# Decoder step on one Trainium2 core: squares folded to one tile, output tiles rescaled on VectorE, normalised tiles made in portions

## The chip, the core and the metric

The kernel runs on one core of a Trainium2 chip. Five engines work side by side, each with its own queue: TensorE (PE; its weight loads are listed apart as PEld) multiplies matrices into PSUM, VectorE (DVE), ScalarE (ACT) and GpSimd (POOL) do elementwise work, and SyncE (SP) issues the DMAs. An engine works off its queue in order and waits at an instruction until its inputs are there and its output buffer is free. The metric is the device time of one execution in microseconds (us); the profile shows one execution.

## The reference

One step of a decoder layer for 256 prompt tokens and 8 x 4 sample tokens, 288 tokens in all, with 2048 features. What matters here is the first half:

```python
mod = (silu(c) @ w_ada + b_ada)            # per request: sh_m, sc_m, gt_m, sh_f, sc_f, gt_f
h = rms(x, g_mix) * (1 + sc_m) + sh_m      # rms: x * rsqrt(mean(x*x) + EPS) * gain
proj = h @ w_in                            # 2048 -> 9216 columns (72 tiles of 128)
b_gate, c_gate, hc, u, v, ga, gb = split(proj)
...
```

Behind that come a short convolution, a spatial gate, a merge through three more weight matrices, a second rms and a SwiGLU of width 5632. Everything is float32.

## The kernel before, in words

Activations lie with features on the 128 partitions and the 288 tokens along the free axis: 16 tiles of x, one for each 128 features. For precision each operand is split into a high part (`hi`, a cast on ScalarE) and a low part (`lo`, a subtraction on VectorE), and each product is made of three matmuls (`triple`, L217 to L219). Weight blocks come by DMA into seven buffers `raw`, and `Blk.split` (L390 to L406) makes hi and lo of four 128x128 tiles at a time into four buffers each.

The product with w_in is done in passes over parts of the 16 contraction tiles. Blocks `wA` (nine, each eight output tiles) take tiles 0 and 1 for all 72 outputs; `wB` tiles 2 to 4 and `wX` tiles 5 to 7 for outputs 48 to 71; `wC` (24 blocks, two outputs each, six contraction tiles) tiles 2 to 7 for outputs 0 to 47; `wD` the last eight tiles. The partial sums are kept in SBUF and added to by the sinks (`sinkA` to `sinkD`), which also free the PSUM buffer of the output tile; there are four such buffers.

The root of the mean square isn't known when the first pass starts. So the first ROOTLESS = 32 outputs are made from x times (1 + sc_m) x gain, without the root (`mk_xe`, `xe`), with ten more columns: the shift and scale vectors `mod` as nine columns and one of padding, 298 in all (`TU`). Once the root is known (`S["rb1"]`, the root spread over the partitions), these 32 tiles are multiplied by it and get the shift of their sample requests (`rescale`, on POOL); the shift of the prompt is added in `sinkC`. Outputs from 32 on use `h1`, which contains the root.

The modulation `mod` comes from `Ada` blocks (aA: contraction over w_ada, four blocks of 1 MB; aC, aD, aE in between the others later). Ahead of them and between them stand idle matmuls (`warm`) on a constant tile.

`squares1` squares x in five pieces on ScalarE and adds them on VectorE down to six tiles of 288 tokens. `sums1` sums each over the partitions by matmuls with a column of ones (L514), three for each tile, and `roots` makes the root. `norm1` spreads it (L206, L527) and makes h1[0] and h1[1] at once (`mk_h1(0, 2)`). The squares' instructions are hung up in a table of slots (i, j), "after output tile j of block wA[i]", which `paced` works off, with the splits of the next weights in its even slots. `later(f, gap)` puts work behind a number of `triple`s.

The order on TensorE is the program's throughout. On ScalarE, VectorE and SyncE it is the program's until `head.close()` at wA[3]; behind that a planner sets the order of all engines but TensorE. SyncE issues loads in order, seven blocks ahead. Each load waits there until its buffer is free.

Of the kernel before, what the change touches and what calls it, by code (L numbers as in the profile page):

```python
# [1 line left out]

# [1 line left out]

# [16 lines left out]
NC = 9  # L21
# [22 lines left out]


TB = (0, 128, 160)
ROOTLESS = 32
LATER = 48
XCUT = (0, 2, 6, 10, 14, 16)

# [35 lines left out]
def _body(tc, nc, d, pc, pw, pslot, ptmp, pps):  # L86
# [289 lines left out]
    class Blk(Step):  # L376
# [10 lines left out]

        cut, width, outer, pace = None, T, False, None

        def split(self, most=99):  # L390
            n = self.nk * self.nm
            nseg = -(-n // SEG)
            per = -(-n // nseg)
            self.parts = self.parts or []
            for s in range(len(self.parts), n, per):
                if most == 0:
                    return
                most -= 1
                e = min(n, s + per)
                w = (e - s) * 128  # L400
                hi = pw.tile([P, w], F32R, tag="hi", name=nm("hi"), bufs=SPB, padded_shape=[P, SEG * 128])
                A.copy(hi, self.raw[:, s * 128 : e * 128])  # L402
                lo = pw.tile([P, w], F32R, tag="lo", name=nm("lo"), bufs=SPB, padded_shape=[P, SEG * 128])
                V.tensor_tensor(lo, self.raw[:, s * 128 : e * 128], hi.bitcast(F32), ALU.subtract)  # L404
# [73 lines left out]
    def warm(n):  # L478
        for _ in range(n):
            PE.matmul(idle[:, :T], wb[:, :P], wb, start=True, stop=True)  # L480

    def squares1():
        qa, qb = (pw.tile([P, 2048], F32, tag="raw", name=nm("q"), bufs=RAW) for _ in range(2))
        for q in (qa, qb):
            G.memset(q[:, 7 * T : 7 * T + 1], 0.0)

        def part_of(q, o, n):
            return q[:, o * T : (o + n) * T].rearrange("p (k t) -> p k t", t=T)

        q1, q0, q2, q4 = part_of(qa, 0, 4), part_of(qa, 4, 2), part_of(qb, 0, 4), part_of(qb, 4, 2)  # L490

        def square(q, i):
            return lambda: A.activation(q, x[:, XCUT[i] : XCUT[i + 1], :], AF.Square)

        def add(o, q):
            return lambda: V.tensor_tensor(o, o, q, ALU.add)
# [12 lines left out]
    def sums1():  # L509
        got = S["r1"] = {"ps": psmisc()}  # L510
        qs = S.pop("sq")
        for i, q in enumerate(qs):
            for tb, o in enumerate(TB):
                PE.matmul(  # L514
                    got["ps"][:, tb : tb + 1],
                    q[:, o : o + 128],
                    ones[:, 0:1],
                    start=i + tb == 0,
                    stop=False,
                    skip_group_check=True,  # L520
                )
        roots(got, D, False, False)

    def norm1():
        ps = rstd_bcast(S["r1"])
        S["rb1"] = ptmp.tile([P, T], F32, tag="rb", name=nm("rb"), bufs=1)
        A.copy(S["rb1"], ps)  # L527
        mk_h1(0, 2, False).run()

    h1, xe = {}, {}  # L530

    def mk_xe():
        end = tmp(2 * (TU - TP)).rearrange("p (k t) -> p k t", k=2)
        V.memset(end[:, :, T + NC - TP :], 0.0)

        def scaled(k):
            hi = slot(F32R, (P, TU))
            A.activation(hi[:, :TP], x[:, k, :TP], AF.Copy, scale=gm1[:, k, 0:1])
            lo = slot(F32R, (P, TU))
            xe[k] = (hi, lo)  # L540

        def ends(k):
            V.tensor_tensor(sam(end[:, k, : T - TP]), sam(x[:, k, TP:]), bc4(gm1[:, k, 1:]), ALU.mult)
            V.tensor_copy(end[:, k, T - TP : T - TP + NC], mod[:, k, :])
            V.tensor_copy(xe[k][0][:, TP:], end[:, k, :])
# [8 lines left out]
        def weights(n):  # L554
            wA[0].split(n)
# [30 lines left out]
    def sinkA(m, ps):  # L586
        t = slot(shape=(P, TU) if m < ROOTLESS else (P, T))
        part[m] = t[:, :T]
        w = T
        if m < ROOTLESS:  # L590
            raws[m], w = t, TU
        if m % 2:
            A.copy(t[:, :w], ps[:, :w])  # L593
        else:
            V.tensor_copy(t[:, :w], ps[:, :w])  # L595

    def rescale(m0, m1):
        def f():
            for m in range(m0, m1):
                t = raws[m]  # L600
                G.tensor_tensor(t[:, :T], t[:, :T], S["rb1"], ALU.mult)  # L601
                G.tensor_tensor(sam(t[:, TP:T]), sam(t[:, TP:T]), bc4(t[:, T + 1 : T + NC]), ALU.add)

        return Do(f, None)

    def sinkC(m, ps):
        if m not in raws:
            return sinkB(m, ps)
        t = raws.pop(m)
        V.scalar_tensor_tensor(t[:, :TP], ps[:, :TP], t[:, T : T + 1], t[:, :TP], ALU.add, ALU.add)  # L610
        V.tensor_tensor(t[:, TP:T], ps[:, TP:T], t[:, TP:T], ALU.add)

    def sinkB(m, ps):
        V.tensor_tensor(part[m], ps[:, :T], part[m], ALU.add)  # L614


    ya, yb, u2 = {}, {}, {}
# [18 lines left out]
    def mix_conv(j):  # L636
        b, c, hc = part.pop(j), part.pop(8 + j), part.pop(16 + j)
        z = tmp()
        V.tensor_tensor(z, c, hc, ALU.mult)
# [3 lines left out]
        V.tensor_copy(zs[:, :, 0:2], state[:, j])  # L643
# [203 lines left out]
    wX = [Blk("wX", i, rh1, lambda m, ps: sinkB(LATER + m, ps)) for i in range((72 - LATER) // 4)]  # L847
# [23 lines left out]
    plan = {2: [Do(root, None)], 6: aC[:4], 8: aC[4:] + [mk_h1(2, 5)]}  # L871
    for i in range(4):
# [52 lines left out]
    load_x(0)  # L925
    stream[4].load(512)
    S["paced"] = squares1()
    stream[5].load()
    load_x(1)
    load_x(2)  # L930
    stream[6].load()
    load_x(3)
    load_x(4)
    SY.dma_start(cp, d["cpack2"])
    blks = [s for s in stream if isinstance(s, Blk)]
    nxt, cur = 0, 0
    for s in steps:
        if s is wA[3]:
            head.close()
        if isinstance(s, Do):  # L940
            if pending and s.gap is not None:
# [130 lines left out]
```

## Time and profile before

| what | us |
|---|---|
| median of three runs | 1662.79 (1661.29 to 1664.73) |
| the profiled execution, as timed | 1665.84 |
| its span, first to last instruction | 1664.0 |
| TensorE busy | 1643.4 |
| VectorE busy | 998.5 |
| ScalarE busy | 740.1 |
| POOL busy | 59.5 |

The span is what the profile divides into shares; the timed figure of the same execution holds 1.84 us more around it. A busy TensorE need not be one at full rate, since matmuls overlap and its clock can be granted at half; the views by stretches therefore give the granted clock with each stretch. In the rows of a timeline the first two numbers are start and duration in us; what stands in brackets is the idle time ahead and what ended it. In a line's own view the three numbers are least, median and most ns of one instruction.

### The profile page before, as it was taken

How to read it: one execution, taken by the hardware profiler on the slowest of the kernel's cores; microseconds unless marked ns; L12 is line 12 of the kernel's file. 1: busy time of each engine (PE TensorE's matmuls, PEld its weight loads, DVE VectorE, ACT ScalarE, POOL GpSimd, SP SyncE). 2: the span in 40 equal slices, each digit the busy share in tenths (PEclk: the TensorE clock that was granted, in tenths of full speed). 3: DMA queues.
4: the chain of work that ended last, by engine and by line, in shares of the span. 5: the costliest groups of instructions: out<-in, count | busy, mean ns of one | idle time of the engine just before them, and what ended most of it. 6: DMA issues, size and time to landing. Idle time of an engine off the chain costs nothing.

```text
span 1664.0 us, 31217 instructions
## 1 busy us (share of the span) xinstructions
PE 1643.4 (99%) x12466; PEld 1568.3 (94%) x12466; DVE 998.5 (60%) x2087; ACT 740.1 (44%) x1355; POOL 59.5 (4%) x128
## 2 busy tenths in 40 slices
PE   9999999999999999999999999999999999999997
PEld 7888989999989998999989999999999999999997
DVE  4567656877755566567844455555555555555565
ACT  4344334653434434446734444444444444344453
POOL 0720000000000000002000000000000000000000
PEclk9899999999999999999999999999999999999998
DMA  9478776766688656764477546453464534644341
GB/s 349 143 302 322 299 294 208 266 250 253 255 306 317 242 215 253 283 223 162 146 299 304 207 157 220 155 175 120 157 221 163 174 117 156 217 173 164 115 154 57
DMA packets 59281, 357.59 MB, mean 215 GB/s; under 512 B 6624, under 2 KB 9600, under 8 KB 28288
## 3 DMA queue, kind: packets, MB, share of 16 engines
q1 hardware_dynamic: 58848, 355.38, 58.7%
q8 instruction: 97, 1.59, 0.4%
q14 instruction: 48, 0.39, 0.1%
q10 hardware_dynamic: 288, 0.22, 0.1%
HBM read 352.49 MB, written 3.09 MB: 214 GB/s over the span
## 4 chain that ended last, share of the span: by engine, by line
issue 51%; PE 46%; DVE 2%; ACT 0%; POOL 0%; POOLq 0%; DVEq 0%; ACTq 0%
PE pm L217 13%; PE pm L218 13%; PE pm L219 13%; PE ada L333 4%; PE pm L480 1%; DVE lo L404 1%; PE px L514 0%; DVE x L828 0%; PE px L358 0%; ACT hi L402 0%; DVE s L269 0%; DVE s L250 0%; PE px L715 0%; PE px L717 0%; PE px L675 0%
## 5 line engine op out<-in xcount | busy, mean ns | idle before, releaser
L217 PE MATMUL pm<-s,hi 128*128 128x288 f32 (+1 forms) x3760 | 1113.6, 296 | 6.0 <-ACT s L593 4.4
L218 PE MATMUL pm<-s,hi 128*128 128x288 f32 (+1 forms) x3760 | 1110.2, 295 | 0.5 <-DVE s L269 0.3
L219 PE MATMUL pm<-s,lo 128*128 128x288 f32 (+1 forms) x3760 | 1110.4, 295 | 0.0
L404 DVE TENSOR_TENSOR lo<-raw,hi 128x512 fp32r<-128x512 f32 (+1 forms) x960 | 658.8, 687 | 504.3 <-ACT hi L402 489.9
L402 ACT CAST hi<-raw 128x512 fp32r<-128x512 f32 (+1 forms) x960 | 587.8, 613 | 816.4 <-PE pm L218 793.6
L217 PEld LDWEIGHTS pm<-s,hi 128*128 128x128 f32 x3760 | 708.5, 188 | 25.8 <-issue 16.1
L218 PEld LDWEIGHTS pm<-s,hi 128*128 128x128 f32 x3760 | 707.7, 188 | 1.4 <-DVE s L552 0.7
L219 PEld LDWEIGHTS pm<-s,lo 128*128 128x128 f32 x3760 | 708.0, 188 | 0.0
L333 PE MATMUL ada<-raw,cs 128*32 128x512 f32 (+2 forms) x832 | 88.2, 563 | 0.0
L333 PEld LDWEIGHTS ada<-raw,cs 128*32 128x32 f32 x832 | 24.2, 109 | 46.1 <-issue 44.5
L197 POOL TENSOR_TENSOR r<-e,mhalf 128x3 f32<-128x3 f32 x4 | 3.4, 855 | 1149.5 <-DVE e L196 1102.5
L622 DVE TENSOR_TENSOR s<-pm,s 128x288 f32<-128x288 f32 x72 | 32.9, 457 | 15.7 <-PE pm L219 15.6
L614 DVE TENSOR_TENSOR s<-pm,s 128x288 f32<-128x288 f32 x64 | 29.1, 455 | 19.2 <-PE pm L219 17.9
L245 DVE TENSOR_TENSOR s<-t,s 128x288 fp32r<-128x288 f32 (+1 forms) x76 | 34.6, 459 | 6.9 <-ACT s L243 6.9
L243 ACT CAST s<-t 128x288 fp32r<-128x288 f32 (+1 forms) x76 | 32.6, 433 | 13.6 <-DVE t L654 6.4
L285 DVE SCALAR_TENSOR_TENSOR x<-pm,mod,x 128x256 f32<-128x256 f32 x80 | 38.0, 475 | 0.0
L601 POOL TENSOR_TENSOR s<-s,rb 128x288 f32<-128x288 f32 x32 | 29.3, 916 | 4.2 <-ACT rb L527 4.2
L800 DVE SCALAR_TENSOR_TENSOR t<-t,pm 128x288 f32<-128x288 f32 x42 | 19.1, 454 | 16.7 <-PE pm L219 16.7
L284 DVE TENSOR_TENSOR t<-pm,mod 128x32 f32<-128x32 f32 x80 | 15.3, 192 | 21.2 <-PE pm L219 21.2
L595 DVE COPY s<-pm 128x288 f32<-128x288 f32 (+1 forms) x36 | 16.2, 456 | 12.1 <-PE pm L219 12.1
L156 ACT ACTIVATE t<-x 128x288 f32<-128x288 f32 x30 | 13.3, 445 | 20.8 <-DVE x L286 20.8
L593 ACT COPY s<-pm 128x288 f32<-128x288 f32 (+1 forms) x36 | 14.2, 399 | 16.8 <-PE pm L219 16.8
(119 smaller groups left out, 495.7 us busy)
## 6 DMA issues: line engine op xcount, KB each, us to landing
raw<-in_fi SPq DMA_DIRECT2D x84, 1024.0 KB, 4.8
raw<-in_a SPq DMA_DIRECT2D x64, 1024.0 KB, 9.7
raw<-in_f SPq DMA_DIRECT2D x64, 704.0 KB, 4.1
raw<-in_wD SPq DMA_DIRECT2D x36, 1024.0 KB, 4.9
raw<-in_wC SPq DMA_DIRECT2D x24, 768.0 KB, 5.1
raw<-in_aE SPq DMA_DIRECT2D x16, 1024.0 KB, 9.7
raw<-in_wo SPq DMA_DIRECT2D x16, 1024.0 KB, 4.9
raw<-in_pa SPq DMA_DIRECT2D x8, 1024.0 KB, 4.9
```

What stands on the lines that cost most here:

```text
L217: PE.matmul(out, wh, ah, start=first, stop=False)
L218: PE.matmul(out, wh, al, start=False, stop=False)
L219: lh = PE.matmul(out, wl, ah, start=False, stop=last)
L243: A.copy(hi, a)
L245: V.tensor_tensor(lo, a, hi.bitcast(F32), ALU.subtract)
L285: V.scalar_tensor_tensor(x[:, m, :TP], ps[:, :TP], mod[:, gt0 + m, 0:1], x[:, m, :TP], ALU.mult, ALU.add)
L333: PE.matmul(acc[32 * j : 32 * j + 32, :w], cs[:, kt, :], self.raw[:, o : o + w], start=(kt < ks), stop=(kt >= 16 - ks), tile_position=(0, ...
L402: A.copy(hi, self.raw[:, s * 128 : e * 128])
L404: V.tensor_tensor(lo, self.raw[:, s * 128 : e * 128], hi.bitcast(F32), ALU.subtract)
L601: G.tensor_tensor(t[:, :T], t[:, :T], S["rb1"], ALU.mult)
L614: V.tensor_tensor(part[m], ps[:, :T], part[m], ALU.add)
L622: V.tensor_tensor(a, ps[:, :T], a, ALU.add)
```

## The change

- The squares: x's five pieces are squared from slot (0, 1) on, and three further additions on VectorE fold everything to one tile of 288 tokens. `sums1` then makes three matmuls in place of 18.
- ROOTLESS goes from 32 to 40: block wA[4] too is made without the root, with 298 columns.
- The rescaling leaves POOL. VectorE does it in the long pass: behind each eviction of wC's output m the tile m + 4, the first four behind the last evictions of wX. `behind` ties the order to the eviction.
- h1[0] and h1[1] are made in portions in slots (3, 3) to (4, 1), in place of at once in `norm1`.
- `sinkA` gives one more eviction of eight to ScalarE. In `mk_xe` the low part of the first weights is put behind the first low part of x, and the cast of the last columns goes to ScalarE; the second tile's two small instructions go to POOL.
- Idle matmuls: 24, 8, 6, 6 and 7 where 36, 10, 14, 16 and 10 stood, and four between the halves of aA[3].
- aC and h1(2 to 5) come one block earlier. Loads of x's pieces move ahead among those of wA[1] and wA[2]. The program's own order holds until wA[5].

```diff
-ROOTLESS = 32
+ROOTLESS = 40
...
+    def behind(a, b):
+        tc.add_manual_dep(
+            a.ins,
+            b.ins.name,
+            mybir.DependencyInfo(mybir.DependencyClass.NoSync, mybir.DependencyReason.DATA),
+            reason="program order",
+        )
...
-        S["sq"] = [q1[:, i] for i in range(4)] + [q4[:, i] for i in range(2)]
+        S["sq"] = q1[:, 0]
         return {
-            (0, 5): square(q0, 0),
-            (1, 1): square(q1, 1),
-            (1, 3): add(q1[:, 0:2], q0),
-            (1, 4): square(q2, 2),
-            (1, 6): add(q1, q2),
-            (2, 1): square(q2, 3),
-            (2, 3): lambda: (square(q4, 4)(), add(q1, q2)()),
+            (0, 1): square(q0, 0),
+            (0, 3): square(q1, 1),
+            (0, 4): add(q1[:, 0:2], q0),
+            (0, 6): square(q2, 2),
+            (1, 0): add(q1, q2),
+            (1, 2): square(q2, 3),
+            (1, 3): square(q4, 4),
+            (1, 5): add(q1, q2),
+            (2, 1): add(q1[:, 0:2], q1[:, 2:4]),
+            (2, 3): add(q1[:, 0:2], q4),
+            (2, 5): add(q1[:, 0], q1[:, 1]),
+            (3, 3): lambda: (scale1(0), affine1(0)),
+            (3, 5): lambda: (scale1(1), high1(0), affine1(1)),
+            (3, 7): lambda: (low1(0), high1(1)),
+            (4, 1): lambda: low1(1),
         }
 
     def sums1():
         got = S["r1"] = {"ps": psmisc()}
-        qs = S.pop("sq")
-        for i, q in enumerate(qs):
...
+        square_sum(got["ps"], S.pop("sq"), 0, True, True)
         roots(got, D, False, False)
...
-        mk_h1(0, 2, False).run()
...
-        aA[3].tail(0, lambda: gm_of(0, 2), lambda: weights(1))
-        for f in (scaled, ends):
-            f(0)
-        rest(0)
-        scaled(1)
-        ends(1)
+        low = []
+        aA[3].tail(0, lambda: gm_of(0, 2), lambda: wA[0].split(1, low))
+        scaled(0)
+        ends(0, V)
+        scaled(1)
+        rest(0)
+        low[0]()
+        ends(1, G)
         rest(1)
-        weights(1)
+        wA[0].split(1)
...
-        if m % 2:
+        if m % 2 or m % 8 == 4:
             A.copy(t[:, :w], ps[:, :w])
...
-    def rescale(m0, m1):
-        def f():
-            for m in range(m0, m1):
-                t = raws[m]
-                G.tensor_tensor(t[:, :T], t[:, :T], S["rb1"], ALU.mult)
-                G.tensor_tensor(sam(t[:, TP:T]), sam(t[:, TP:T]), bc4(t[:, T + 1 : T + NC]), ALU.add)
...
-        V.tensor_tensor(t[:, TP:T], ps[:, TP:T], t[:, TP:T], ALU.add)
+        rescale(m + 4, V.tensor_tensor(t[:, TP:T], ps[:, TP:T], t[:, TP:T], ALU.add))
+
+    def rescale(m, after):
+        if m in raws:
+            t = raws[m]
+            behind(V.tensor_tensor(t[:, :T], t[:, :T], S["rb1"], ALU.mult), after)
+            V.tensor_tensor(sam(t[:, TP:T]), sam(t[:, TP:T]), bc4(t[:, T + 1 : T + NC]), ALU.add)
+
+    def sinkX(m, ps):
+        after = sinkB(m, ps)
+        if m >= 68:
+            rescale(m - 68, after)
...
+    aA[3].half = lambda: warm(4)
...
-    wA[0].cut, wA[1].cut, wA[2].cut, wA[3].cut = 512, 1024, 1024, 1024
+    wA[0].cut = 512
+    wA[1].cut = wA[2].cut = wA[3].cut = wA[4].cut = 1024
...
-    steps = [Do(lambda: warm(36)), aA[0], Do(lambda: warm(10)), aA[1], Do(lambda: warm(14)), aA[2], Do(lambda: warm(16)), aA[3]]
-    steps += [Do(mk_xe), Do(lambda: warm(10))]
+    steps = [Do(lambda: warm(24)), aA[0], Do(lambda: warm(8)), aA[1], Do(lambda: warm(6)), aA[2], Do(lambda: warm(6)), aA[3]]
+    steps += [Do(mk_xe), Do(lambda: warm(7))]
 
     def root():
-        later(sums1, 10)
-        later(norm1, 6)
+        later(sums1, 13)
+        later(norm1, 7)
 
-    plan = {2: [Do(root, None)], 6: aC[:4], 8: aC[4:] + [mk_h1(2, 5)]}
-    for i in range(4):
-        plan[5 + i] = [rescale(8 * i, 8 * i + 8)] + plan.get(5 + i, [])
+    plan = {2: [Do(root, None)], 5: aC[:4], 7: aC[4:] + [mk_h1(2, 5)]}
...
     load_x(1)
+    stream[5].load(0, 1024)
     load_x(2)
-    stream[6].load()
+    stream[5].load(1024)
     load_x(3)
     load_x(4)
+    stream[6].load()
...
-        if s is wA[3]:
+        if s is wA[5]:
             head.close()
```

The helpers of the portions, in the new code: `scale1(k)` multiplies x[k] by the root on VectorE, `affine1(k)` applies scale and shift (the prompt's part on ScalarE, the sample's on VectorE), `high1(k)` casts on ScalarE, `low1(k)` subtracts on VectorE. In `mix_conv` the first small copy is tied `behind` the product that precedes it.

More of the change, by code (lines that the diff above doesn't have):

```diff
@@ L1 @@
 import contextlib
+import functools
 import numpy as np
@@ L388, in _body, with split @@
         cut, width, outer, pace = None, T, False, None
-        def split(self, most=99):
+        def split(self, most=99, low=None):
             n = self.nk * self.nm
@@ L403, in split @@
                 lo = pw.tile([P, w], F32R, tag="lo", name=nm("lo"), bufs=SPB, padded_shape=[P, SEG * 128])
-                V.tensor_tensor(lo, self.raw[:, s * 128 : e * 128], hi.bitcast(F32), ALU.subtract)
+                sub = functools.partial(
+                    V.tensor_tensor, lo, self.raw[:, s * 128 : e * 128], hi.bitcast(F32), ALU.subtract
+                )
+                if low is None:
+                    sub()
+                else:
+                    low.append(sub)
                 for i in range(e - s):
@@ L510, in sums1 @@
         got = S["r1"] = {"ps": psmisc()}
-        qs = S.pop("sq")
-        for i, q in enumerate(qs):
[L513 to L521, printed above, removed]
+        square_sum(got["ps"], S.pop("sq"), 0, True, True)
         roots(got, D, False, False)
@@ L527, in norm1, with scale1, affine1, high1 @@
         A.copy(S["rb1"], ps)
-        mk_h1(0, 2, False).run()
+    first1 = {}
+    def scale1(k):
+        first1[k] = normed(k, S["rb1"])
+    def affine1(k):
+        t, h = first1[k], tmp()
+        A.activation(h[:, :TP], t[:, :TP], AF.Identity, bias=mod[:, k, 0:1], scale=gm1[:, k, 0:1])
+        V.tensor_tensor(sam(h[:, TP:]), sam(t[:, TP:]), bc4(gm1[:, k, 1:]), ALU.mult)
+        V.tensor_tensor(sam(h[:, TP:]), sam(h[:, TP:]), bc4(mod[:, k, 1:]), ALU.add)
+        first1[k] = h
+    def high1(k):
+        hi = slot(F32R)
+        A.copy(hi, first1[k])
+        first1[k] = (first1[k], hi)
+    def low1(k):
+        h, hi = first1.pop(k)
+        lo = slot(F32R)
+        V.tensor_tensor(lo, h, hi.bitcast(F32), ALU.subtract)
+        h1[k] = (hi, lo)
     h1, xe = {}, {}
@@ L540, in scaled, with ends @@
             xe[k] = (hi, lo)
[L542 to L545, printed above, removed]
+        def ends(k, E):
+            E.tensor_tensor(sam(end[:, k, : T - TP]), sam(x[:, k, TP:]), bc4(gm1[:, k, 1:]), ALU.mult)
+            E.tensor_copy(end[:, k, T - TP : T - TP + NC], mod[:, k, :])
+            A.copy(xe[k][0][:, TP:], end[:, k, :])
         def rest(k):
@@ L610, in sinkC @@
         V.scalar_tensor_tensor(t[:, :TP], ps[:, :TP], t[:, T : T + 1], t[:, :TP], ALU.add, ALU.add)
-        V.tensor_tensor(t[:, TP:T], ps[:, TP:T], t[:, TP:T], ALU.add)
+        rescale(m + 4, V.tensor_tensor(t[:, TP:T], ps[:, TP:T], t[:, TP:T], ALU.add))
[8 more added lines that the diff above has]
+            rescale(m - 68, after)
     def sinkB(m, ps):
-        V.tensor_tensor(part[m], ps[:, :T], part[m], ALU.add)
+        return V.tensor_tensor(part[m], ps[:, :T], part[m], ALU.add)
     ya, yb, u2 = {}, {}, {}
@@ L638, in mix_conv @@
         z = tmp()
-        V.tensor_tensor(z, c, hc, ALU.mult)
+        made = V.tensor_tensor(z, c, hc, ALU.mult)
         V.tensor_copy(zout[:, j, 0:2], z[:, TP - 2 : TP])
@@ L642, in mix_conv @@
         zs = ptmp.tile([P, NB, 6], F32, tag="zs", name=nm("zs"), bufs=2)
-        V.tensor_copy(zs[:, :, 0:2], state[:, j])
+        behind(V.tensor_copy(zs[:, :, 0:2], state[:, j]), made)
         V.tensor_copy(zs[:, :, 2:], sam(z[:, TP:]))
@@ L844, in _body @@
     aA[3].defer = True
+    aA[3].half = lambda: warm(4)
     wA = [Blk("wA", i, (xe if i < ROOTLESS // 8 else h1).__getitem__, sinkA) for i in range(9)]
     wB = [Blk("wB", i, rh1, lambda m, ps: sinkB(LATER + m, ps)) for i in range((72 - LATER) // 4)]
-    wX = [Blk("wX", i, rh1, lambda m, ps: sinkB(LATER + m, ps)) for i in range((72 - LATER) // 4)]
+    wX = [Blk("wX", i, rh1, lambda m, ps: sinkX(LATER + m, ps)) for i in range((72 - LATER) // 4)]
     wC = [Blk("wC", i, rh1, sinkC) for i in range(LATER // 2)]
@@ L860, in paced @@
         return f
[L862 removed]
+    for i in range(5):
         wA[i].pace = paced(i)
[L864 to L865 removed]
+    steps = [Do(lambda: warm(24)), aA[0], Do(lambda: warm(8)), aA[1], Do(lambda: warm(6)), aA[2], Do(lambda: warm(6)), aA[3]]
+    steps += [Do(mk_xe), Do(lambda: warm(7))]
     def root():
[L868 to L873 removed]
+        later(sums1, 13)
+        later(norm1, 7)
+    plan = {2: [Do(root, None)], 5: aC[:4], 7: aC[4:] + [mk_h1(2, 5)]}
     steps += at(wA, plan)
```

4 lines of the change are left out of this document (removed).

## The prediction

> **What bounds the kernel now.** I read the page's table of engines first, then the waits of the whole span, then busy time by stretches, last the rows of the stretches that lose time.
>
> ```profile
> PE 1643.4 (99%) x12466; PEld 1568.3 (94%) x12466; DVE 998.5 (60%) x2087; ACT 740.1 (44%) x1355; POOL 59.5 (4%) x128
> PE pm L217 <- ACT s L593: 4.4, 2, 2.3
> PE px L514 <- DVE q L496: 1.6, 1, 1.6
> PE pm L217 <- DVE s L595: 1.3, 1, 1.3
> ```
>
> TensorE (PE) is busy for 99% of the span. The three lower rows are most of what it waited for (us in total, times, longest), and all of it lies ahead of 104 us. So the time is that of TensorE's own work plus what the first hundred microseconds lose. Busy isn't full speed, so the stretches count (columns: PE, weight load, VectorE, ScalarE, POOL, each with records; granted clock; DMA share; GB/s):
>
> ```profile
> 20.25:21.71 1.46, 1.24 (x4) 0.64 (x4) 1.43 (x8) 1.30 (x3) 0.00 (x0) 1.00 1.02 409
> 21.71:38.60 16.89, 16.89 (x122) 16.83 (x122) 12.88 (x25) 12.15 (x24) 0.00 (x0) 1.00 0.96 385
> 38.60:40.37 1.77, 0.19 (x2) 0.00 (x0) 1.77 (x3) 1.12 (x3) 0.00 (x0) 1.00 0.19 57
> 40.37:47.91 7.54, 7.54 (x37) 7.54 (x37) 0.92 (x2) 0.00 (x0) 0.00 (x0) 0.52 0.43 141
> 47.91:51.10 3.19, 3.19 (x15) 3.19 (x15) 0.16 (x1) 1.44 (x3) 0.86 (x1) 0.52 0.92 343
> 51.10:61.00 9.90, 6.25 (x44) 5.61 (x42) 9.79 (x16) 4.81 (x11) 7.78 (x12) 1.00 0.35 121
> 61.00:65.08 4.08, 4.08 (x19) 4.08 (x20) 1.92 (x4) 0.93 (x2) 4.08 (x9) 0.58 0.00 0
> 65.08:103.20 38.12, 36.04 (x295) 31.92 (x293) 26.06 (x51) 20.29 (x45) 27.77 (x45) 1.00 0.68 256
> 160.00:291.00 131.00, 131.00 (x1005) 122.62 (x1004) 80.69 (x183) 50.38 (x84) 0.00 (x0) 1.00 0.73 274
> ```
>
> From 21.71 to 38.60 TensorE is dense: 122 matmuls of 298 columns in 16.89 us, 0.138 each. From 38.60 to 65.08 it is not: a wait, 36 sum matmuls in 7.54 us at a clock of 0.52, matmuls at half clock, two more waits, half clock again. From 65.08 on only one wait of 2.08 us is left.
>
> **The change part by part.** Everything is taken off this profiled execution: span 1664.0, 1665.84 as timed; the median of the runs shown is 1662.79. I work out a difference and apply it to the median.
>
> *The front.* The rows show ada's last block (L333) behind 16 idle matmuls, and the chain from it to the first products:
>
> ```profile
> 14.46 2.13 PE L480 MATMUL pm<-wb 128*128 128x288 bf16 x16
> 15.52 1.53 SPq L132 DMA_DIRECT2D x<-in_x  x2
> 16.52 1.07 PE L333 MATMUL ada<-raw,cs 128*32 128x256 f32 x16
> 17.51 0.96 SPq L386 DMA_DIRECT2D raw<-in_wA  x2
> 17.93 0.62 ACT L402 CAST hi<-raw 128x512 fp32r<-128x512 f32 x1
> 18.58 0.69 DVE L404 TENSOR_TENSOR lo<-raw,hi 128x512 fp32r<-128x512 f32 x1 [11.94 <-ACT hi L402]
> 19.19 0.17 DVE L362 TENSOR_TENSOR mod<-px,cp 128x18 f32<-128x18 f32 x1
> 20.25 0.37 PE L217 MATMUL pm<-s,hi 128*128 128x298 f32 x1 [0.31 <-ACT s L538]
> 21.71 0.41 PE L218 MATMUL pm<-s,hi 128*128 128x298 f32 x1
> SPq L132 <- DMA raw<-in_aA: 0.9, 1, 0.9
> ```
>
> SP's load at 15.52 had waited for a piece of aA to land (last row), by the order of issue the last one: ada's end was 1.0 us later than its data. Fewer idle matmuls (24, 8, 6, 6, four of another batch between aA[3]'s halves, 7, where 36, 10, 14, 16 and 10 stood) let the first half run before 15.5 and the second at 15.5, ending near 16.05, not 17.59. What comes next is x: the load at 17.51 waits, by the same order, for x's first piece. The low part of the weights (0.69 at 18.58) no longer stands ahead of mod on VectorE, so mod and gm are ready about when x is, at 17.5; ScalarE's scaled tile then takes until 18.1 and the first product starts near 18.2. Then VectorE's queue sets the pace: one low part (0.48 + 0.20), the weights' low part 0.69, the second tile's 0.48 + 0.20; dense from about 19.9, not 21.71. Taken: **-1.8**. Bounds: -1.0 (ada's lateness alone) and -2.05 (all of 20.25 to 18.2).
>
> *Squares and sums.* Blocks 0 to 3 of wA hold 192 matmuls; four lie before 21.71. 188 x 0.138 = 25.9 us, but they take 21.71 to 65.08, 43.4 us. So **17.4 us** there are no products. The parts:
>
> ```profile
> 36.65 1.17 ACT L493 ACTIVATE q<-x 128x1152 f32<-128x1152 f32 x1
> L514 PEld LDWEIGHTS px<-ones,q x36: 186/333/337, 40.4 to 47.5; 128*128 128x128 f32 x36
> 51.77 0.94 PE L206 MATMUL px<-cp,r 128*128 128x128 f32 x6
> 58.51 0.19 PEld L217 LDWEIGHTS pm<-s,hi 128*128 128x128 f32 x1 [2.54 <-ACT s L593]
> 60.97 0.19 PEld L217 LDWEIGHTS pm<-s,hi 128*128 128x128 f32 x1 [1.59 <-DVE s L595]
> 40.70:50.95 10.25, 10.25 (x48) 10.25 (x48) 0.75 (x2) 1.30 (x3) 0.86 (x1) 0.50 0.57 197
> 54.30:57.70 3.40, 1.91 (x14) 1.67 (x13) 3.33 (x7) 2.43 (x5) 3.40 (x7) 1.00 0.89 308
> 57.70:61.14 3.44, 1.28 (x7) 1.04 (x8) 3.44 (x6) 1.07 (x4) 3.44 (x5) 1.00 0.01 2
> 61.14:64.60 3.46, 3.46 (x15) 3.46 (x16) 1.75 (x4) 0.93 (x2) 3.46 (x7) 0.51 0.00 0
> ```
>
> Wait for the squares 1.77; sums 7.54; 13 matmuls at half clock to 51.1, 0.11 too slow each, 1.4; the broadcast (L206) 0.86 until the next product; waits of 2.46 and 1.5 around 58.51 and 60.97; 14 more matmuls at half clock, 1.5. Sum 17.0.
>
> Afterwards the sums are three matmuls, six records. At full clock a weight load of a sum takes 186 ns, at half clock 333 (min and median above); 7.54/36 = 0.209 each becomes 0.209 x 186/333 = 0.117, six are 0.7, with a handover 0.9. Folding adds three VectorE sums of at most 576 columns. Squares start a block earlier, so ScalarE's lateness (the square at 36.65 just before the sums) goes; what is late next is VectorE's last addition. Its slot follows tile 5's eviction; on VectorE it stands behind a weight low part, which waits for ScalarE's copy of tile 4 (0.41) and cast (0.62). From tile 4's end: cast done at 0.9, low part 0.95 to 1.55, addition to 2.0; TensorE asks 1.24 after it. Wait **0.8**; bounds 0 and 1.77 as now. The broadcast stays, 0.86. Left 0.8 + 0.9 + 0.86 = 2.6, so **-14.8** if the two waits of 4.0 go and the clock stays up.
>
> *h1's first two tiles in portions.* Same instructions, now spread over slots of blocks 3 and 4 in place of one lump. That lump blocked the evictions, and it was slow beside POOL:
>
> ```profile
> L250 DVE TENSOR_TENSOR s<-x,rb x15: 447/451/1066, 53.3 to 299.8; 128x288 f32<-128x288 f32 x15
> L263 DVE TENSOR_TENSOR t<-t,mod x13: 181/189/732, 55.6 to 299.0; 128x32 f32<-128x32 f32 x13
> L601 POOL TENSOR_TENSOR s<-s,rb x32: 792/807/1342, 53.2 to 91.5; 128x288 f32<-128x288 f32 x32
> ```
>
> The maxima, 1066 and 732, are those issued beside L601; the medians are 451 and 189. With POOL idle and four PSUM buffers, each filled in 0.83, a portion of at most 0.45 + 0.19 + 0.19 delays no eviction by three tiles. Waits 0; bounds 0 and 4.0. ScalarE gets three squares and a fifth eviction in block 0: evictions 5 x 0.41, casts 4 x 0.62, squares 0.69 + 1.17 + 1.17, 7.6 us in a block of 6.6, but in row 21.71:38.60 24 such instructions took 12.15 busy, overlapping; cover is the same four buffers.
>
> *Wider blocks.* Block 4 gets 298 columns: 48 x 0.138 x 10/298 = **+0.2**. Loads of x are moved ahead of wA[1], wA[2]; a block of 1 MB per 6.6 us is 158 GB/s against 385 moved in 21.71:38.60, so nothing waits for them. POOL loses 64 instructions that nothing on TensorE waited for.
>
> *Rescaling in the long pass.* 40 tiles get two VectorE instructions, 36 of them behind the evictions of wC (18 matmuls, 2.4 us a tile), four in wX. Today:
>
> ```profile
> 235.42 0.69 DVE L404 TENSOR_TENSOR lo<-raw,hi 128x512 fp32r<-128x512 f32 x1 [0.90 <-ACT hi L402]
> 236.03 0.48 DVE L610 SCALAR_TENSOR_TENSOR s<-pm,s 128x256 f32<-128x256 f32 x1
> 236.42 0.18 DVE L611 TENSOR_TENSOR s<-pm,s 128x32 f32<-128x32 f32 x1
> 243.80:252.80 9.00, 9.00 (x70) 9.00 (x70) 8.78 (x33) 6.99 (x14) 0.00 (x0) 1.00 0.91 364
> ```
>
> Starts lie 0.61 apart behind a low part and 0.39 behind an eviction. A tile costs 1.5 x 0.61 + 0.39 + 0.11 = 1.42 of 2.4; the rescale, by L250 and L263 less the same overlap, 0.38 + 0.10 = 0.48: 1.9 of 2.4, 79%. Queued behind a rescale is the next low part, late by 0.5; four hi/lo buffers of 1.58 us each stand ahead of TensorE. Cost **0**. The tight place is 243.8 to 252.8, where h1(8 to 16) already fills VectorE to 8.78 of 9.0 while TensorE stays dense; four rescales add 1.9 there. Bounds 0 and +6. Tiles 32 to 39 split an eviction in two, +0.1 each, covered likewise; `behind` only fixes an order.
>
> The Trainium skill, "VectorE: DVE Perf Modes", section "The DRAIN you can't avoid", says a VectorE instruction doesn't start before the pipe of the one before is empty (an unheld one, it adds, starts earlier). By whole durations a tile would be an estimated 2.34 of 2.4, nearly full, against this change. The trace has 0.61 and 0.39 between starts of instructions that take 0.69 and 0.48, so it doesn't agree here.
>
> *h1(2 to 5)* moves a block earlier with the same instructions; its 2.08 wait stays, bounds 0 and 2.1.
>
> **Sum:** -1.8 - 14.8 + 0.2 = -16.4. 1662.8 - 16.4 = **1646.4**.
>
> **The rivals.**
> 1. *The clock falls once more at the sums.* Window 54.30:57.70 had 1.5 us without matmuls and kept its clock; 57.70:61.14 had 2.1 and lost it for the next 3.46 us, and the sums at 40.70:50.95 didn't bring it back. Mine would have 0.8 + 0.9 = 1.7 at worst in one such window, close. Price 1.7 for a window, 3.4 with the sums and broadcast in it: 1648 to 1650. The Trainium skill, "TensorE: Matmul & The Clock Gate", Part 1, has the clock halve only after a whole idle window of about 3.4 us; by that it stays, and the forecast holds. The trace shows it falling on 2.1, so it differs.
> 2. *A wait less:* the 2.08 of h1(2 to 5), perhaps the 0.8: 1643.5 to 1644.4.
> 3. *VectorE is late in the long pass,* around h1(8 to 16): +2 to +6, 1648 to 1652.
> 4. *Folding doesn't do what it says:* the last addition is so late that waits eat the sums' gain; with 6.8 and 1.4 given back, 1654 to 1655.
> 5. *Slower:* rescaling costs VectorE what it cost beside POOL, 1.07 + 0.73 = 1.8 a tile. Then 1.42 + 1.8 exceeds 2.4 by 0.8, 36 times 29 us: 1675. It turns at 0.98 + 16.4/36 = 1.44 a tile. Against it: POOL is 0.00 in 160:291.
>
> **How the numbers follow.** Forecast 0.50, clock 0.22, a wait less 0.12, VectorE late 0.08, folding 0.05, slower 0.03. The range takes in the first three and most of the fourth, with the front's bounds: 1643 to 1652. A measurement tells about 0.2%, 3.3 us; only the fifth rival is slower, and the fourth with a late front could come within: faster 0.94, same 0.03, slower 0.03.
>
> **What would show it.** Right: first product near 18.2 and dense from 20; six sum records within 1 us at a clock near 1.0; block 4 starting near 48.4; no POOL work but the root; wX and wC dense. Wrong: a second stretch at a clock of 0.5, waits of TensorE on evictions in blocks 0 to 4, or waits on L404's low part in wC, above all where h1(8 to 16) is made.

## The result and the profile after

| | median us | ratio to before, 95% interval |
|---|---|---|
| before, at the time of the prediction | 1662.79 (3 runs; 1662.85 with the fourth that the first ratio uses) | |
| forecast | 1646.4 (1643 to 1652) | 0.990 |
| changed kernel | 1654.12 (1652.70 to 1655.13, 4 runs) | 0.9946 (0.9929 to 0.9964) |
| changed kernel once more | 1654.43 (1653.57 to 1654.98, 5 runs) | 0.9937 (0.9925 to 0.9950) |
| before, beside it | 1664.93 (1660.86 to 1666.47, 15 runs) | |

The change is faster, by 8.7 us in the first comparison and 10.5 in the second; both intervals lie below 1. 16.4 were forecast, and the time lies above the range.

The profiled execution after it: 1652.70 as timed, span 1650.9. First its engines and five of the waits of TensorE over the whole span (us in total, times, longest):

```profile
PE 1632.5 (99%) x12405; PEld 1556.5 (94%) x12405; DVE 1007.4 (61%) x2165; ACT 742.7 (45%) x1366; POOL 20.1 (1%) x66
PE pm L218 <- ACT s L627: 2.1, 1, 2.1
PE px L207 <- POOL r L198: 1.4, 1, 1.4
PE ada L342 <- DMA raw<-in_aA: 1.3, 2, 0.7
PE px L182 <- DVE q L511: 0.9, 1, 0.9
PE pm L220 <- DVE lo L417: 0.5, 2, 0.3
```

The two waits of the lump ahead of 61 us are gone, the wait for the folded squares is 0.9 (0.8 was forecast), and the 2.1 us for h1(2 to 5) stayed, as forecast. The second row (1.4) stands in both profiles, at the end of the span. The line numbers have moved: 217 to 219 are 218 to 220, 404 is 417, 514 is 182, 493 is 508, 496 is 511, 593 is 627, 206 is 207, 333 is 342.

The stretches of the start, same columns as before:

```profile
20.23:32.80 12.57, 12.57 (x92) 12.57 (x92) 8.43 (x14) 9.76 (x19) 0.00 (x0) 1.00 1.03 409
32.80:36.60 3.80, 3.12 (x19) 2.38 (x18) 3.32 (x6) 2.99 (x7) 0.00 (x0) 1.00 1.01 409
39.95:40.86 0.91, 0.03 (x1) 0.00 (x0) 0.86 (x2) 0.59 (x2) 0.00 (x0) 1.00 0.52 155
40.86:41.69 0.83, 0.83 (x7) 0.83 (x8) 0.00 (x0) 0.00 (x0) 0.00 (x0) 1.00 0.99 415
44.68:45.46 0.78, 0.78 (x7) 0.62 (x6) 0.29 (x1) 0.41 (x1) 0.00 (x0) 1.00 1.02 431
45.46:57.36 11.90, 11.90 (x88) 11.56 (x92) 8.49 (x20) 8.64 (x20) 0.00 (x0) 1.00 0.48 157
```

The granted clock is 1.00 throughout; the sums take 0.83 us where 7.54 stood. The first product stands at 18.61 (18.2 forecast), dense products begin at 20.23, not 21.71 (19.9 forecast), and block 4 begins at 50.4 (48.4 forecast). New is the second row: from 32.8 to 36.6 only 19 matmuls ran where 27 fit.

Where the gain is can be read off landmarks on TensorE. The chain in order of time has the first group of aD, which both kernels reach after the same products, at

```profile
115.43 2.72 PE ada L333 x32
```

in the kernel before and at

```profile
101.07 2.72 PE ada L342 x32
```

in the changed one. So the start gained 14.4 us. At the end of the span only 13.1 are left (1664.0 and 1650.9): 1.3 us were given back behind the start, where TensorE has the same waits in both kernels. And between the medians it is 8.7. There are three questions: 2.0 us missing in the start (by block 4 they are missing already), 1.3 lost behind it, and 4.4 between profile and medians.

### The profile page after: what moved, and what is told of

The parts are those of the page before. It is cut to its first block, busy times and chain, and to the rows that moved or that the text cites. A ratio compares the mean times of both kernels' runs of the same rounds, so it can differ in the third digit from the quotient of the medians.

```text
span 1650.9 us, 31102 instructions
## 1 busy us (share of the span) xinstructions
PE 1632.5 (99%) x12405; PEld 1556.5 (94%) x12405; DVE 1007.4 (61%) x2165; ACT 742.7 (45%) x1366; POOL 20.1 (1%) x66
## 4 chain that ended last, share of the span: by engine, by line
issue 52%; PE 45%; DVE 2%; ACT 1%; DMA 1%; SPq 0%; POOLq 0%; POOL 0%; DVEq 0%; ACTq 0%
PE pm L218 13%; PE pm L220 13%; PE pm L219 13%; PE ada L342 4%; DMA raw<-in_aA 1%; DVE lo L417 1%; DVE x L864 0%; PE px L367 0%; ACT hi L411 0%; SPq L324 0%; PE px L751 0%; PE px L753 0%; PE px L711 0%; ACT q L508 0%; DVE q L511 0%
## 5 line engine op out<-in xcount | busy, mean ns | idle before, releaser
L658 DVE TENSOR_TENSOR s<-pm,s 128x288 f32<-128x288 f32 x72 | 32.8, 456 | 15.8 <-PE pm L220 15.6
L650 DVE TENSOR_TENSOR s<-pm,s 128x288 f32<-128x288 f32 x56 | 25.4, 455 | 16.1 <-PE pm L220 14.9
L627 ACT COPY s<-pm 128x298 f32<-128x298 f32 (+1 forms) x45 | 17.9, 403 | 12.0 <-PE pm L220 12.0
L635 DVE SCALAR_TENSOR_TENSOR s<-pm,s 128x256 f32<-128x256 f32 x40 | 19.2, 480 | 5.1 <-PE pm L220 5.1
L162 DVE TENSOR_TENSOR acc<-acc,t 128x288 f32<-128x288 f32 x34 | 15.5, 455 | 8.2 <-ACT t L157 8.2
L371 DVE TENSOR_TENSOR mod<-px,cp 128x36 f32<-128x36 f32 (+2 forms) x26 | 3.5, 186 | 27.8 <-PE px L367 27.7
## 6 DMA issues: line engine op xcount, KB each, us to landing
raw<-in_aE SPq DMA_DIRECT2D x16, 1024.0 KB, 10.5
```

Source lines behind the costliest of these rows:

```text
L650: return V.tensor_tensor(part[m], ps[:, :T], part[m], ALU.add)
L658: V.tensor_tensor(a, ps[:, :T], a, ALU.add)
```

## The experiments

All ratios are to the kernel before on the same chip. "First aD" is the landmark above in each profile, "rest" the span less that.

| run | median us | ratio (interval) | first aD | span | rest |
|---|---|---|---|---|---|
| before (first profile) | 1662.79 | | 115.43 | 1664.0 | 1548.6 |
| b1: before again | 1665.05 | 1.0000 (0.9991 to 1.0009) | 114.98 | 1663.6 | 1548.6 |
| changed (first profile) | 1654.12 | 0.9946 (0.9929 to 0.9964) | 101.07 | 1650.9 | 1549.8 |
| a1: changed again | 1654.43 | 0.9937 (0.9925 to 0.9950) | 101.15 | 1651.8 | 1550.7 |
| u_fold | 1657.42 | 0.9955 (0.9940 to 0.9970) | 106.59 | 1656.8 | 1550.2 |
| v_fold | 1654.41 | 0.9943 (0.9928 to 0.9959) | 103.44 | 1652.7 | 1549.3 |
| u_war | 1652.43 | 0.9931 (0.9917 to 0.9944) | 99.83 | 1650.2 | 1550.4 |
| u_pool | 1658.49 | 0.9965 (0.9952 to 0.9978) | 106.75 | 1656.7 | 1550.0 |
| u_port | 1654.13 | 0.9937 (0.9922 to 0.9952) | 102.14 | 1650.7 | 1548.6 |
| u_warm | 1655.03 | 0.9945 (0.9928 to 0.9962) | 101.77 | 1651.7 | 1549.9 |
| d_slot91 | 1655.03 | 0.9944 (0.9930 to 0.9959) | 102.84 | 1654.0 | 1551.2 |
| d_dve | 1653.55 | 0.9938 (0.9923 to 0.9953) | 101.63 | 1652.1 | 1550.5 |
| n_h1 | 1648.58 | 0.9908 (0.9893 to 0.9922) | 98.74 | 1646.8 | 1548.1 |
| best1 | 1646.94 | 0.9901 (0.9883 to 0.9919) | 96.53 | 1644.7 | 1548.2 |

### b1 and a1: both kernels again

> The kernel before, once more, five rounds and a new profile. Its profiled execution was 3.0 us above its median, and my sum was taken off that execution. Theory P (phase of the clock's windows): other executions of it have fewer or shorter half-clock stretches between 38 and 65 us, so the first ada group behind wA (77.94 us in the first profile) comes 1.5 to 4 us earlier here and the mean clock lies above 0.992. Theory Q (pace): the start is as in the first profile within 0.3 us, and executions differ in the dense part alone, by some 0.2% of matmul pace.

> The changed kernel, once more, five rounds and a new profile. Both theories: no stretch at half clock around the sums; its first ada group behind wA within 0.4 us of 57.36. Theory P: times spread less than those of the kernel before, by a clock that stays up; ratio near 0.995. Theory Q: spread as wide as before's, from the dense part.

The new execution of the kernel before, by stretches:

```profile
40.37:51.10 10.73, 10.45 (x49) 10.45 (x50) 1.36 (x4) 1.42 (x3) 0.86 (x1) 0.54 0.58 203
61.14:64.60 3.46, 3.46 (x28) 3.46 (x27) 2.30 (x5) 1.86 (x4) 3.46 (x6) 1.00 0.00 0
101.00:104.50 3.50, 3.29 (x19) 3.30 (x20) 2.50 (x6) 1.41 (x5) 0.00 (x0) 0.75 0.90 377
104.50:108.00 3.50, 3.50 (x22) 3.50 (x22) 1.98 (x4) 1.50 (x3) 0.00 (x0) 0.77 0.67 238
```

The wait ahead of the last two stretches in b1, and the first of them in the first profile, which has its wait of 2.08 us in it:

```profile
101.20 0.40 PE L217 MATMUL pm<-s,hi 128*128 128x288 f32 x1 [2.08 <-ACT s L593]
```

```profile
101.00:104.50 3.50, 1.42 (x11) 1.30 (x10) 2.85 (x8) 2.43 (x7) 0.00 (x0) 1.00 1.01 420
```

At 61.14 the clock is up in b1; in the first profile it was 0.51 there, with 15 records in place of 28. In its place it falls behind the wait of h1(2 to 5), 0.75 and 0.77 from 101 to 108, where the first profile had 1.00. The first aC group comes 2.0 us earlier, and by the first aD 0.45 are left of that. So which of the waits costs a stretch at half clock changes from execution to execution: theory P. The times go with it: of b1's eleven executions the fastest has 1661.18 us at a mean clock of 0.994, the slowest 1666.34 at 0.991. 0.003 of 1664 us are 5.0 (the clock is given to three digits, so 3.3 to 6.7), and the times differ by 5.2. a1 has its first aC group at 57.35, as expected, and its five executions lie within 1.4 us at 0.996 to 0.997; the first four of the changed kernel lay within 2.4. Theory Q, as the reason for the spread, falls: the dense matmuls behind the start take the same time in both profiles of the kernel before (table under d_slot91). A difference of pace is there all the same, but between the kernels.

### u_fold and v_fold: the folding undone, and alone

In u_fold:

```diff
-        S["sq"] = q1[:, 0]
+        S["sq"] = [q1[:, i] for i in range(4)] + [q4[:, i] for i in range(2)]
...
-            (2, 1): add(q1[:, 0:2], q1[:, 2:4]),
-            (2, 3): add(q1[:, 0:2], q4),
-            (2, 5): add(q1[:, 0], q1[:, 1]),
...
-        square_sum(got["ps"], S.pop("sq"), 0, True, True)
+        for i, q in enumerate(S.pop("sq")):
+            for tb, o in enumerate(TB):
+                PE.matmul(got["ps"][:, tb : tb + 1], q[:, o : o + 128], ones[:, 0:1], start=i + tb == 0, stop=False, skip_group_check=True)
```

v_fold is the kernel before with the changed table of squares, its `sums1` and `later(sums1, 13)`, nothing else.

> The changed kernel with the folding undone: six tiles of squares are summed by 18 matmuls, and the last three additions on VectorE are left out. My sum: 30 more sum records at 0.117 us if the clock stays up, +3.5 us, less the wait of 0.9 us for the last addition: +2.6. If the long low-activity stretch of sums drags the clock to half as in the kernel before: +7 to +9 us. Rival: folding is worth nothing since TensorE waits for the additions instead: 0 to +1.

> The kernel before with the folding alone: squares in the changed kernel's slots, three more additions, three sum matmuls; the root's parts three products later. Rescaling on POOL, h1's lump, idle matmuls and loads as before. Folding as the main term: the sums shrink from 7.5 us to 0.8, and the clock stays up around them: -7 to -9 us. The waits of the lump beside POOL stay, 3 to 4 us, and may cost a stretch at half clock of their own. Rival: the additions come so late that TensorE waits instead: -1 to -4.

Undoing it costs 5.4 us at the first aD (3.0 between the medians), between the two figures expected: the clock does fall, but late and for less long than in the kernel before. u_fold by stretches:

```profile
40.70:44.00 3.30, 3.30 (x26) 3.30 (x25) 0.00 (x0) 0.00 (x0) 0.00 (x0) 0.78 0.44 158
44.00:47.50 3.50, 3.50 (x16) 3.50 (x17) 1.23 (x3) 0.00 (x0) 0.85 (x1) 0.50 0.86 299
47.50:51.00 3.50, 3.50 (x20) 3.34 (x20) 1.07 (x2) 1.40 (x4) 0.00 (x0) 0.73 0.52 215
```

The 18 sums are one run of 36 records from 39.91 to 45.20 us, and they wait for nothing:

```profile
39.91 5.29 PE L533 MATMUL px<-ones,q 128*128 128x1 f32 x36
```

So here the clock falls (0.78, then 0.50) while TensorE counts as busy and no wait stands before it: in this kernel a long run of sum matmuls, one moving column each, loses the clock by itself. The three sums of the changed kernel, 0.83 us, ran at 1.00.

Alone, the folding makes the kernel before 9.2 us faster, nearly all that the whole change brings. Its start gains 12.0 us of the change's 14.4. The lump beside POOL still makes TensorE wait, but for 2.0 us, not the 3 to 4 expected, and that costs no clock in this profile:

```profile
50.58 0.41 PE L217 MATMUL pm<-s,hi 128*128 128x298 f32 x1 [1.97 <-ACT s L587]
51.00:54.30 3.30, 3.30 (x26) 3.30 (x26) 2.92 (x6) 1.86 (x4) 3.30 (x6) 1.00 0.00 0
```

### u_war: a buffer that is read while it is to be written

```diff
-            (1, 2): square(q2, 3),
-            (1, 3): square(q4, 4),
-            (1, 5): add(q1, q2),
+            (1, 2): square(q4, 4),
+            (1, 4): square(q2, 3),
+            (1, 6): add(q1, q2),
```

The rows behind it, from the timeline of the changed kernel (start, duration, in brackets the idle time before):

```profile
28.95 1.35 DVE L511 TENSOR_TENSOR q<-q,q 128x1152 f32<-128x1152 f32 x1
30.38 1.17 ACT L508 ACTIVATE q<-x 128x1152 f32<-128x1152 f32 x1 [1.23 <-issue]
33.28 0.69 DVE L417 TENSOR_TENSOR lo<-raw,hi 128x512 fp32r<-128x512 f32 x1 [2.00 <-ACT hi L411]
33.30 0.41 PE L218 MATMUL pm<-s,hi 128*128 128x298 f32 x1 [0.19 <-ACT hi L411]
34.02 0.41 PE L220 MATMUL pm<-s,lo 128*128 128x298 f32 x1 [0.18 <-DVE lo L417]
36.27 0.41 PE L220 MATMUL pm<-s,lo 128*128 128x298 f32 x1 [0.32 <-DVE lo L417]
```

The fourth piece's squares go into q2, which VectorE adds from 28.95 to 30.30. ScalarE stands for 1.23 us and starts at 30.38; the profile names no releaser. Behind it stand the evictions and the casts of the next weights, and TensorE waits for these. VectorE, idle for 2.00 us meanwhile, isn't the cause.

> The changed kernel with two slots swapped: in block 1 the fifth piece is squared at output 2 and the fourth, which writes the buffer that the addition at output 0 reads, at output 4, its addition at output 6. Theory W: the square of the fourth piece held ScalarE 1.23 us for that buffer, and the three late weight halves at 33.3, 34.0 and 36.3 us follow from it: those waits (1.5 us together) go, -1.0 to -1.5 us by the profile. Rival: they come from VectorE's additions being too many for blocks 1 and 2; then the waits stay, 0.

The stretch in u_war:

```profile
32.80:36.60 3.80, 3.80 (x29) 3.70 (x28) 3.32 (x5) 2.61 (x6) 0.00 (x0) 1.00 1.00 405
36.60:41.00 4.40, 3.19 (x24) 2.95 (x23) 3.12 (x8) 1.76 (x4) 0.34 (x1) 1.00 0.53 184
```

29 records in place of 19, none of the three waits; the wait ahead of the sums grows from 0.9 to 1.2. First aD 1.3 us earlier: theory W.

### u_pool, u_port, u_warm: one part undone each

u_pool has the `rescale` of the kernel before (POOL, eight tiles at a time) behind blocks 3 to 7 of wA. u_port leaves out the slots (3, 3) to (4, 1) and ends `norm1` with `mk_h1(0, 2, False).run()`. u_warm has `warm` 36, 10, 14, 16 and 10 and no `half`.

> The changed kernel with the rescaling of its 40 tiles back on POOL, eight tiles behind each of blocks 3 to 7 of wA, and none of it in the long pass; the moving operands of the later passes lie at the same addresses as in the changed kernel. Theory V (VectorE has room): moving the rescaling is worth nothing in the long pass; POOL beside the portions of h1 costs 0 to 1.5 us ahead of 60 us. Matmul pace in wC: by theory A (the addresses of the moving operands set it) 133.0 ns as in the changed kernel; by theory D (VectorE's rescaling slows TensorE's reads) back to 132.2 ns, -0.7 us over wX and wC.

> The changed kernel with h1's first two tiles made at once when the root is spread, not in portions; POOL stays idle. My sum charged 4.0 us of waits to the lump and to POOL beside it together. If the lump alone makes the waits: +2 to +4 us. If POOL beside it made them: 0 to +1 us.

> The changed kernel with the idle matmuls of the kernel before (36, 10, 14, 16 and 10, none between the halves of the last ada block). My sum: ada ends 1.0 to 1.5 us later, first product 0.8 to 1.3 us later, and the time with it. Rival: x's first piece (17.5 us) and VectorE's chain hide it, 0 to +0.4 us.

u_pool costs 4.1 us between medians, more than either theory had. The portions lose 1.0 us by POOL beside them (first aC 58.33 and 57.35), as expected; the rest comes later, beside h1(2 to 5), where POOL now still works. TensorE's longest wait of u_pool, and its stretches:

```profile
86.02 0.61 PE L218 MATMUL pm<-s,hi 128*128 128x288 f32 x1 [4.59 <-ACT s L627]
84.00:92.00 8.00, 5.98 (x29) 5.98 (x30) 4.83 (x9) 3.17 (x8) 8.00 (x15) 0.57 0.34 141
```

4.59 in place of 2.08, and half clock behind it. Its matmul pace in wC is that of the changed kernel (132.97 ns in both, table below), although VectorE rescales nothing there: theory D falls.

u_port's start is 1.0 us later: the lump alone costs no more (one wait of 0.5 us). POOL beside the portions costs 1.0 too, and both together make v_fold wait 2.0. So neither has the 4.0 us to itself, and in kernels without the half clock at the sums they don't reach 4.0 together; b1, too, waits only 1.57 and 1.36 us there. u_port's time is none the less that of the changed kernel, since its rest is 2.1 us shorter (1.3 by its pace, 0.75 by the broadcast at the end; both are under d_slot91). u_warm's start is 0.6 us later, under the 0.8 expected: part of ada's lateness stays hidden. Behind what (x's landing is the guess) wasn't tested.

### d_dve: a third instruction in each rescale

```diff
             behind(V.tensor_tensor(t[:, :T], t[:, :T], S["rb1"], ALU.mult), after)
+            V.tensor_tensor(t[:, :T], t[:, :T], ones[:, 0:1].to_broadcast([P, T]), ALU.mult)
```

> The changed kernel with a third VectorE instruction of 288 columns in each rescale, a product with ones, 40 times 0.45 us; same addresses. VectorE would then be at 1.42 + 0.48 + 0.38 = 2.28 of 2.4 us a tile in wC. Theory V (VectorE has room, as forecast): 0 to +1 us. Rival: VectorE's lateness passes to TensorE, above all where h1(8 to 16) is made: +3 to +10 us.

0.9 us less than a1 between medians, within the spread; rest 1550.5 against 1550.7. TensorE has the wait of 2.1 us for h1(2 to 5), and behind it only the two at the end of the span (0.7 and 1.4) that every profile has. VectorE has room even with 18 us more. This is also against the sentence of the Trainium skill ("VectorE: DVE Perf Modes", "The DRAIN you can't avoid") weighed in the prediction, where it is taken without its exception: by whole durations a tile would now be an estimated 2.34 + 0.45 = 2.8 of 2.4 us, and 36 tiles some 14 us late.

### d_slot91: the same program with its operands elsewhere

```diff
-SLOTS = 92
+SLOTS = 91
```

> The changed kernel with 91 activation buffers in place of 92, so that nearly all moving operands lie elsewhere; nothing else differs. Theory A: the pace of dense matmuls changes by some tenths of a ns, by sections and not alike in all (wC, wD, the last passes), and the time by up to 2 us either way, with the start as in the changed kernel. Theory D or one of instructions: pace as in the changed kernel, 133.0 in wC and 132.5 in the last passes.

The built programs give the address of every operand; no trace shows it. Behind the start the weights of all products with 288 columns lie at the same addresses in every kernel here. Their moving operands (hi and lo of the activations) don't: 46% lie in the changed kernel where they lay before, because buffers come free in another order. Between the changed kernel, u_war, u_fold, u_pool, u_warm and d_dve all of them agree, between n_h1 and best1 too; d_slot91 shares 4% with the changed kernel. The PSUM tiles lie in the same four banks, half of them in another one of the four before and after the change. u_fold and u_warm differ from the changed kernel in this as well, and not in their pace.

Behind the first aD all kernels have the same products in the same order. The table takes 10 534 pairs of neighbours among them whose starts lie less than 0.16 us apart in every profile, so that no wait is in it: the sum of their distances, and the mean in three sections.

| | sum, us | wC, ns (200 to 284 us in a1) | wD, ns (420 to 500) | last passes, ns (1200 to 1300) |
|---|---|---|---|---|
| before (first profile), b1 | 1393.36, 1393.36 | 132.3 | 132.6 | 132.1 |
| changed (first profile), a1 | 1395.47, 1395.58 | 133.0 | 132.3 | 132.4 |
| u_fold, u_war, u_pool, u_warm, d_dve | 1395.55 to 1395.60 | 133.0 | 132.3 | 132.4 |
| d_slot91 | 1395.72 | 133.3 | 133.0 | 132.2 |
| u_port | 1394.26 | 133.0 | 132.3 | 132.1 |
| v_fold | 1394.07 | 132.2 | 132.6 | 132.3 |
| n_h1, best1 | 1393.65, 1393.61 | 132.6 | 131.9 | 132.1 |

Kernels with one set of addresses have one pace in each section, whatever VectorE does beside; d_slot91 has another, slower in wC and wD and faster in the last passes. That is theory A. It costs the changed kernel 2.1 us in every one of its seven profiles. Which property of an address sets the pace stays open.

The column "rest" moves by one thing more. The last six matmuls of a profile, the broadcast of the last root, stand behind a wait of 1.4 us, and their clock differs from execution to execution. The kernel before, then the first profile of the changed one:

```profile
1653.08:1654.87 1.79, 1.78 (x6) 1.42 (x6) 0.00 (x0) 0.00 (x0) 0.00 (x0) 0.50 0.00 0
```

```profile
1640.70:1641.79 1.09, 1.09 (x6) 0.84 (x6) 0.00 (x0) 0.00 (x0) 0.00 (x0) 0.89 0.00 0
```

This gave the changed kernel's first profile 0.7 us back by luck; in a1 the broadcast takes 1.79 us, as in both profiles of the kernel before. So the 1.3 us lost behind the start are 2.1 of pace less that 0.7, to within 0.2. It also spreads the rests of the seven profiles, 1549.8 to 1550.7 us, with broadcasts of 1.04 to 1.79.

d_slot91's start was expected to be that of the changed kernel, and isn't: its first aD stands at 102.84, and a1's at 101.15. Both wait 2.1 us for h1(2 to 5), until 82.80 and 82.53; d_slot91 loses the clock behind it, while a1 has 1.00 there, with 56 records:

```profile
82.00:90.00 8.00, 7.21 (x43) 7.21 (x44) 4.21 (x9) 4.08 (x10) 0.00 (x0) 0.79 0.47 168
```

### n_h1 and best1: what the wait of h1(2 to 5) is worth

```diff
-    plan = {2: [Do(root, None)], 5: aC[:4], 7: aC[4:] + [mk_h1(2, 5)]}
+    plan = {2: [Do(root, None)], 5: aC[:4], 7: aC[4:] + list(pieces(2, 5))}
```

`pieces` hands out `scale1`, `affine1`, `high1` and `low1` of the three tiles as six steps, four products apart. best1 adds the swap of u_war and `later(sums1, 15)`.

> The changed kernel with h1(2 to 5) made in six pieces, four products apart, over the last two blocks of wA. The wait of 2.1 us of TensorE for an eviction at 82 us goes: the first aD group comes 2.0 us earlier against the first aC group. Time -2 us, and by up to 1.5 us either way from the addresses, which differ in wC and wD.

> n_h1 with the two slots of u_war swapped and the sums two products later. -1.3 us by the swap and up to -1 from the wait for the last addition, beside n_h1's -2: first aC group near 55.2 us, time 1650 to 1651.

From 78 to 86 us the changed kernel (a1) has the first row, n_h1 the second:

```profile
78.00:86.00 8.00, 5.92 (x45) 5.68 (x44) 5.76 (x18) 6.55 (x15) 0.00 (x0) 1.00 0.85 350
```

```profile
78.00:86.00 8.00, 8.00 (x63) 8.00 (x62) 6.93 (x20) 7.28 (x18) 0.00 (x0) 1.00 0.94 367
```

63 records where 45 fit beside a wait. The first aD comes 2.4 us earlier in n_h1 (2.0 expected). That its median lies 5.9 below a1's has two more reasons: a rest shorter by 2.6 us (1.9 by the pace at its addresses, the remainder by the broadcast at the end), and the chip it ran on, where the kernel before took 1663.59 and not 1664.93. By ratio it is 0.9908 against 0.9937. best1 has its first aC at 55.20, and 1646.94 us, 0.9901 of the kernel before: it beats both kernels, and lies below the 1650 to 1651 expected for the same two reasons.

## Why the prediction was wrong

The mechanisms were right, and the sum of what they bring was too high: 16.4 forecast, 13.1 in the two profiles, 8.7 and 10.5 in the medians. That the time falls where rival 4 put it (1654 to 1655) is coincidence: the folding did what it was to do. In the order of the steps:

- **The front: right, a little less.** -1.8 forecast, -1.5 measured (dense from 20.23, not 19.9). The chain ran as worked out, 0.3 to 0.4 late; u_warm gives 0.6 of the gain to the idle matmuls. The rest is put down to the order in `mk_xe`, the weights' low part no longer ahead of mod; no run undoes that alone.
- **Sums, clock and the lump: right in kind.** Sums 0.83 us (0.9 with handover forecast), wait for the last addition 0.9 (0.8), broadcast 0.78 (0.86), clock 1.00, no wait for the lump. v_fold shows the folding as the largest part. The 4.0 us of waits for the lump and POOL belong in part to the execution that was read: b1 waits 2.9 there, and v_fold, which keeps both, 2.0.
- **"ScalarE gets three squares and a fifth eviction in block 0 ... cover is the same four buffers": this step failed.** Busy times were added up for block 0, and the buffers of the squares were left out. In block 1 ScalarE had to wait for VectorE's reading of q2, 1.23 us, and passed it on. u_war puts 1.3 us on it, most of the 2.0 that are missing at block 4. The PSUM buffers did cover late evictions; late weights they do not cover.
- **"Cost 0" for the long pass: right for VectorE, incomplete.** d_dve shows that 18 us more would still fit. But the sum took TensorE's dense part as untouched by the change, a term of nothing, and it became 2.1 us longer by the addresses of the moving operands (1.3 net in the first profile, by the luck of the last broadcast). No row of the profile before could have told the size; that buffers would come free in another order could be seen in the diff.
- **"I work out a difference and apply it to the median": this step cost most in the comparison that was forecast.** The profiled execution of before stood 3.0 us above the median of the three runs, and part of the losses that the sum took away (stretches at half clock) are those by which executions differ, as b1 shows. A difference taken from a slow execution was thus subtracted from a faster one. Against its own execution the sum gives 1649.4, and the changed kernel's profiled execution had 1652.70; its median, in turn, lies 1.4 above that. How much of the 3.0 was chance shows in the fifteen executions beside b1: their median is 1664.93, only 0.9 below the profiled one. Set against that median the forecast would have been 1648.5, and still 5.9 too low. The 1.4 looks like half clock as well: of the changed kernel's nine executions four have a mean clock of 0.997 and 1652.70 to 1653.63 us, five 0.996 and 1654.43 to 1655.13, and 0.001 of 1650 us is 1.65. Both of its profiles are of the first kind, so none shows where the clock is lost; d_slot91 lost it behind the wait of 2.1 us that the change left.

Together: 1646.4 + 3.0 (the base) + 1.4 (the changed kernel's own spread) + 1.3 (q2) + 1.3 (pace, net of the last broadcast) leaves 0.7, of which 0.3 are the front's: 1654.1. The first two are the 4.4 us between profile and medians, the other terms the 3.3 between sum and profile, and 0.4 of those stay unexplained.

The rivals: the clock did not fall at the sums in either profile of the changed kernel, though 0.91 us of waiting and 0.83 us of sums add up to the 1.7 that the first rival named. The wait of 2.1 us stayed, and no rival named it as a place to lose the clock, as d_slot91 did. VectorE was not late. A rival was missing for a TensorE that is slower without waiting, and the range, cut to bounds of waits, did not hold it.

The table of the Trainium skill ("TensorE: Matmul & The Clock Gate", Part 1) gives the half clock after at least one idle window of about 3.4 us. Rows here disagree once more: in b1 the clock fell behind a wait of 2.08 us that ended at 101.20.

## What to carry to other kernels

When a kernel's executions differ by stretches at half clock, work out the losses of a profiled execution against that execution's own time, and ask for a larger sample before the difference is set against a median. When instructions on a nearly full engine are moved, follow the buffers that they write, not the busy time alone: who still reads them, and what stands in the queue behind the wait. And parts that remove the same low-activity stretch don't add up: the folding alone brought 9.2 us here, all else without it 7.5 (u_fold), both together 10.5.

## What was not expected of the hardware

The pace of dense float32r matmuls of 288 columns depends on where the moving operands lie: 131.9 to 133.0 ns a matmul in the same section (wD) over the same products, alike to 0.01 ns in each profile with the same addresses, with all waits absent. Over the 10 534 distances of the table that makes up to 2.4 us (1393.36 to 1395.72), as much as some of the edits are worth. And the clock is lost on less than expected: pauses of 2.1 us cost a stretch at half clock in one execution and none in the next, and in u_fold 36 records of sums in 5.29 us did so without any pause.
